# Gates of three dense tiles scattered into a cleared HBM matrix, in place of one-hot products

## The chip, the cores and the metric

The kernel runs on one core of a Trainium2 chip. The metric is the time of one execution on the device, in microseconds, as the median of a few runs. Engines are called by their names in the profile: PE is TensorE, DVE VectorE, ACT ScalarE, POOL GpSimd, SP SyncE (here a queue that issues DMAs).

## What is computed

One layer of a streaming encoder for 640 tokens: 512 of a prompt and 8 x 16 of running streams, in five tiles of 128 tokens. An attention branch and a gated MLP branch are mixed into the residual; after that comes the part that the change touches, a layer of 16384 small experts ("PEER"). Cut to what matters:

```python
q = (xt @ w_query).reshape(T, PEER_HEADS, 2, PEER_HALF)
s = jnp.einsum('thpd,hpnd->thpn', q, sub_keys)
sv, si = lax.top_k(s, PEER_TOPK)                      # 16 of 128 keys, twice
cand = sv[:, :, 0, :, None] + sv[:, :, 1, None, :]
cand_idx = si[:, :, 0, :, None] * PEER_N_KEYS + si[:, :, 1, None, :]
cv, ci = lax.top_k(cand.reshape(T, PEER_HEADS, 256), PEER_TOPK)
eidx = jnp.take_along_axis(cand_idx.reshape(T, PEER_HEADS, 256), ci, axis=-1)
g = jax.nn.softmax(cv, axis=-1)                       # 8 heads x 16 gates per token
a = jax.nn.gelu(jnp.einsum('thkd,td->thk', expert_u[eidx], xt))
return jnp.einsum('thk,thkd->td', (g * a), expert_v[eidx])
```

So each token has 128 (expert, gate) pairs, 16 in each of 8 heads. The 16 experts of one head are distinct; two heads of a token can pick the same expert, and then both gates count.

## The kernel before

The tiles go in two groups. G1 = (0, 4) takes the gathered way: for each of its tiles 128 indirect DMAs fetch 128 rows of U (8 KB each), a DVE instruction per gather makes the dot products, and 128 more gathers from V are multiplied and added up (`gather_peer`, L721 to L763). That is 512 gathers, all on the POOL queue, spread in the background (`bg`, `tick`) over everything that follows the first query; the rates `RATE_...` say how many per step. G2 = (1, 2, 3) takes the dense way: all 16384 experts are computed for all tokens as products, 32 blocks of 512 experts for U and 64 blocks for V (16 groups of 1024 experts by 4 column blocks), and the activations are multiplied by a matrix of gates, wd[token, expert], which is zero but for 128 entries per token.

The order of the work is: mix of G1, query of G1, mix of G2, query of G2 (four products with `w_q`), then `dense_peer`: LEAD = 12 U blocks first, whose activations are stored to HBM (`ad`), and then groups of V blocks, with further U blocks between them once the stored ones are used up. `gemm` (L190) does every product: it loads weights (`raw`), splits each 128 x 512 piece into a high part on ACT (`whi`, L140) and a low part (`wlo`, L141), and multiplies three times per tile (L206 to L208). The low part is made on DVE; in the two queries every second one is made on POOL (`PLG`, `PLQ` = 2). Small work is put between the steps of `gemm`: `pump` takes pieces from `side`, `tick` from `bg`. A scheduler then sets each engine's order.

The matrix wd is made by `weights` (L767): for each token of a tile, two one-hot matrices are compared out of an iota (the first by 128-digit, times the gate; the second by the lower digit), and their product, contracted over the 128 entries, is that token's 128 x 128 row of wd. Four tokens share a PSUM tile, which ACT copies and SP stores to HBM:

```python
nc.vector.tensor_scalar(a, io128, tr[:, 0, t:t + 1], tr[:, 2, t:t + 1],
                        op0=ALU.is_equal, op1=ALU.mult)
nc.tensor.matmul(pw[:, t - t0, :], a, b, start=True, stop=True)      # L788
nc.sync.dma_start(wd[ti][t0:t0 + 4, :].rearrange("t (i j) -> i t j", i=128), w)
```

One such product is two instructions in the profile, so the three tiles have 768. `routing` (L696) finds the digits beforehand; `h_step` (L801) loads a piece of wd, multiplies it with the activations (L806) and transposes the result for V (L810).

Of the kernel before, what the change touches and what calls it, by code (L numbers as in the profile page):

```python
# [23 lines left out]
SAMPLE = 4  # L24
LEAD = 12
RATE_A = 1.35
RATE_Q = 0.6
RATE_W = 1.2
# [17 lines left out]
ACT_OH = 2  # L46
LOWG = -600
PLG = 2
EL = 4
SP = 1.5  # L50
# [8 lines left out]
def body(tc, A, O):  # L59
    nc = tc.nc  # L60
    with ExitStack() as ctx:
# [34 lines left out]
        def load(src, shape=(128, 512)):  # L96
            t = pools["wk"].tile(list(shape), F32, name=nm("b"), tag="b", bufs=cfg["b"])
            nc.sync.dma_start(t, src)
            return t
# [18 lines left out]
        nc.sync.dma_start(gmix, A["gmix"])  # L118
        kT_all = [slot() for _ in range(2)]
# [65 lines left out]

        def drain():
            while side:
                pump(1)

        def gemm(lhs, k0, K, src, evict, ticks=0, width=512):  # L190
            n = len(lhs)
            accs = [acc() for _ in range(n)]
            for kc in range(K // 2):
# [16 lines left out]
                tick(ticks / 2)  # L210
            for i in range(n):
                evict(i, accs[i])
# [200 lines left out]
        route = {}  # L413

# [22 lines left out]
        nc.sync.dma_start(sinks, A["sinks"])  # L437

        def mix(G, xgT, r1, ticks):
# [51 lines left out]
            for nb in range(4):  # L491
# [4 lines left out]
                gemm(xgT, 0, KC, A["w_in"][BLK_VS + nb], ev_z, ticks)  # L496
            ticks = late_ticks
# [3 lines left out]
            for nb in range(4):  # L501
# [4 lines left out]
                gemm(xgT, 0, KC, A["w_in"][BLK_GB + nb], ev_gb, ticks)  # L506
            hs = [mtile([128, D]) for _ in G]
            for nb in range(4):
                cs = slice(nb * 512, nb * 512 + 512)

                def ev_ga(i, a):
                    nc.scalar.activation(hs[i][:, cs], a, AF.Tanh, scale=h1[i])
                gemm(xgT, 0, KC, A["w_in"][BLK_GA + nb], ev_ga, ticks)

# [63 lines left out]
        def query(G, x2T, r2, x1d, xgd, ticks):  # L578
# [3 lines left out]
            if n == 2:  # L582
                for i, ti in enumerate(G):
                    route[ti] = ([], const.tile([128, 128], F32, name=nm("g")), r2[i], x1d[i], xgd[i])
                    bg.append(gather_peer(ti))
            for nb in range(4):
                sub = load(A["subT"][:, nb * 4:nb * 4 + 4, :], (128, 4, 128))

                def ev_r(i, a):
# [13 lines left out]
                    if n == 2:  # L603
                        side.append(pair_index(R[i], G[i], nb))
                gemm(x2T, 0, KC, A["w_q"][nb], ev_r, ticks)

            def fin():
                for i, ti in enumerate(G):
                    if n == 2:
                        gates(route[ti][1], R[i][2])  # L610
                        yield
                    else:
                        yield from routing(R[i], ti)
            side.append(fin())
# [58 lines left out]
        def pair_index(R, ti, q):  # L673
# [12 lines left out]

        def gates(g, cv):
            gv = g.rearrange("p (h k) -> p h k", h=8)
            nc.vector.tensor_sub(gv, cv, cv[:, :, 0:1].to_broadcast([128, 8, 16]))
            nc.scalar.activation(g, g, AF.Exp)  # L690
            gs = stat(8)
            nc.vector.tensor_reduce(gs, gv, axis=AX.X, op=ALU.add)
            nc.vector.reciprocal(gs, gs)
            nc.vector.tensor_mul(gv, gv, gs.unsqueeze(2).to_broadcast([128, 8, 16]))

        def routing(R, ti):  # L696
            sv, si, cv, ci = R
            sif = stage((128, 8, 2, 16))
            nc.vector.tensor_copy(sif, si)
            abf = stage((128, 2, 8, 16))  # L700
            ijg = stage((128, 3, 128))
            places(ci, abf)
            for p in range(2):
                o = ijg[:, p, :].rearrange("p (h k) -> p h k", h=8)
                for q in range(4):
                    hs = slice(2 * q, 2 * q + 2)
                    lookup(o[:, hs], abf[:, p, hs], sif[:, hs, p, :])
                    yield
            gates(ijg[:, 2, :], cv)
            side.append(weights(ti, ijg))  # L710
            yield
# [53 lines left out]
        wd = {}  # L765

        def weights(ti, ijg):  # L767
            wd[ti] = dr.tile([128, 16384], F32, name=nm("wd"))
            pt = misc((128, 4, 128))
            for c in range(3):  # L770
                nc.tensor.transpose(pt[:, c, :], ijg[:, c, :], ident)
            tr = stage((128, 4, 128))
            nc.scalar.copy(tr[:, 0:3, :], pt[:, 0:3, :])
            nc.vector.tensor_scalar_mul(tr[:, 3, :], tr[:, 1, :], -1.0)
            for t0 in range(0, 128, 4):
                pw = misc((128, 4, 128))
                for t in range(t0, t0 + 4):
                    if t % 2 == 0:
                        ab = slot((128, 4, 128))
                    a, b = ab[:, t % 2 * 2, :], ab[:, t % 2 * 2 + 1, :]  # L780
                    nc.vector.tensor_scalar(a, io128, tr[:, 0, t:t + 1], tr[:, 2, t:t + 1],  # L781
                                            op0=ALU.is_equal, op1=ALU.mult)
                    if t % 4 < ACT_OH:
                        nc.scalar.activation(b, io128, AF.Abs, bias=tr[:, 3, t:t + 1])
                        nc.scalar.activation(b, b, AF.Relu, bias=1.0, scale=-1.0)  # L785
                    else:
                        nc.vector.tensor_scalar(b, io128, tr[:, 1, t:t + 1], None, op0=ALU.is_equal)
                    nc.tensor.matmul(pw[:, t - t0, :], a, b, start=True, stop=True)  # L788
                w = slot((128, 4, 128))
                nc.scalar.copy(w, pw)  # L790
                nc.sync.dma_start(wd[ti][t0:t0 + 4, :].rearrange("t (i j) -> i t j", i=128), w)
# [206 lines left out]
```

## Time and profile before

| | us |
|---|---|
| median of 3 runs | 4015.54 (4014.65 to 4018.94) |
| the profiled execution | 4016.88 |
| its span, first to last instruction | 4015.2 |
| PE busy | 3882.2 (97%) |
| DVE busy | 3179.5 (79%) |
| ACT busy | 1727.2 (43%) |
| POOL busy | 799.2 (20%) |
| DMA, mean rate over the span | 295 GB/s |

Matmuls are pipelined: each lasts some 0.39 us, but the next starts after 0.23 us. So starts that follow each other tell how long PE needs, not the mean duration. The granted clock of PE is 0.989 on average. A line of a helper, such as L140 or L206, stands for the whole kernel; the stretches are told apart by time. The second query runs from about 1553 to 1705 us, the first U blocks from there to 2215 us, the one-hot products from 1850 to 2193 us.

### The profile page before, as it was taken

The numbers are of one execution on the slowest core, as the hardware profiler recorded it, in microseconds if no ns is written. First come the engines' busy times: TensorE is split into PE (matmuls) and PEld (weight loads), VectorE is DVE, ScalarE is ACT, GpSimd is POOL, SyncE is SP. The second block draws the span as 40 slices with busy tenths as digits, with TensorE's granted clock in tenths as the row PEclk, the third lists the DMA queues.
The fourth block names the chain that finished last, engine by engine and source line by source line (L and its number), as shares of the span: only waits on it lengthen the run. The fifth ranks groups of instructions, "written<-read, shape, count | busy, mean of one in ns | idle before, by whom it ended". The sixth has DMA issues, their size and how long they took to land.

```text
span 4015.2 us, 52383 instructions
## 1 busy us (share of the span) xinstructions
PE 3882.2 (97%) x17880; PEld 3173.7 (79%) x17880; DVE 3179.5 (79%) x5470; ACT 1727.2 (43%) x3338; POOL 799.2 (20%) x668
## 2 busy tenths in 40 slices
PE   5999998999999999999999899999999999999998
PEld 4778886877777888878888777778888888888886
DVE  4655768977676886989997788888887878787878
ACT  4665554434444334335666333333333333333333
POOL 0000104132211213310111122122222222122213
PEclk8999999999999999999999999999999999999999
DMA  8656786698877898567998989898888888888887
GB/s 216 209 184 202 252 254 234 232 338 316 299 278 279 322 331 301 178 233 250 359 326 271 347 321 352 326 358 331 321 333 319 333 330 329 324 329 325 327 325 288
DMA packets 334300, 1182.84 MB, mean 295 GB/s; under 512 B 34608, under 2 KB 95184, under 8 KB 267472
## 3 DMA queue, kind: packets, MB, share of 16 engines
q1 hardware_dynamic: 260304, 642.59, 48.3%
q0 software_dynamic: 73728, 536.90, 34.7%
q8 instruction: 141, 2.31, 0.2%
q14 instruction: 127, 1.04, 0.1%
HBM read 1117.69 MB, written 61.67 MB: 294 GB/s over the span
## 4 chain that ended last, share of the span: by engine, by line
PE 75%; DVE 10%; DMA 10%; issue 3%; ACT 1%; SPq 0%; POOL 0%; DVEq 0%; ACTq 0%; POOLq 0%
PE acc L207 23%; PE acc L206 23%; PE acc L208 23%; DVE wlo L141 3%; DMA b<-wd 3%; PE pm L788 2%; DMA gb<-in_U,idx 1%; DVE gb L732 1%; DVE xa L737 1%; DMA raw<-in_w_in 1%; DMA gb<-in_V,idx 1%; DMA raw<-in_w_out 1%; PE pm L810 1%; PE pm L301 1%; DVE S L670 1%
## 5 line engine op out<-in xcount | busy, mean ns | idle before, releaser
L206 PE MATMUL acc<-whi,m 128*128 128x512 f32 (+1 forms) x5232 | 2065.4, 395 | 40.6 <-ACT whi L140 40.6
L207 PE MATMUL acc<-wlo,m 128*128 128x512 f32 (+1 forms) x5232 | 2049.9, 392 | 39.8 <-DVE wlo L141 38.1
L208 PE MATMUL acc<-whi,m 128*128 128x512 f32 (+1 forms) x5232 | 2042.7, 390 | 0.0
L140 ACT CAST whi<-raw 128x512 fp32r<-128x512 f32 (+1 forms) x1888 | 1156.5, 617 | 1999.0 <-PE acc L208 1643.0
L141 DVE TENSOR_TENSOR wlo<-raw,whi 128x512 fp32r<-128x512 f32 (+1 forms) x1824 | 1229.5, 692 | 572.4 <-ACT whi L140 568.3
L207 PEld LDWEIGHTS acc<-wlo,m 128*128 128x128 f32 x5232 | 989.2, 189 | 249.1 <-DVE wlo L141 54.5
L206 PEld LDWEIGHTS acc<-whi,m 128*128 128x128 f32 x5232 | 988.8, 189 | 243.1 <-ACT whi L140 42.8
L208 PEld LDWEIGHTS acc<-whi,m 128*128 128x128 f32 x5232 | 988.4, 189 | 201.0
L732 DVE SCALAR_TENSOR_TENSOR gb<-gb,xa 128x2048 f32<-128x2048 f32 x256 | 586.1, 2289 | 68.6 <-DMA gb<-in_U,idx 61.1
L737 DVE SCALAR_TENSOR_TENSOR xa<-gb,hw,xa 128x2048 f32<-128x2048 f32 x239 | 568.2, 2378 | 48.3 <-DMA gb<-in_V,idx 43.2
L746 POOL DMA_INDIRECT gb<-in_V,idx x239 | 310.1, 1297 | 1226.0 <-ACT whi L140 301.3
L746 POOL DMA_INDIRECT gb<-in_U,idx x256 | 331.2, 1294 | 1103.2 <-ACT whi L140 394.9
L141 POOL TENSOR_TENSOR wlo<-raw,whi 128x512 fp32r<-128x512 f32 x64 | 86.9, 1359 | 248.8 <-ACT whi L140 240.6
L788 PEld LDWEIGHTS pm<-s 128*128 128x128 f32 x768 | 101.1, 190 | 20.3 <-ACT s L785 13.6
L781 DVE TENSOR_SCALAR s<-io,S 128x128 f32<-128x128 f32 x384 | 115.9, 345 | 1.1 <-DMA wd<-s 1.1
L839 DVE TENSOR_TENSOR s<-s,acc 128x512 f32<-128x512 f32 x180 | 112.9, 681 | 3.3 <-PE acc L208 3.3
L788 PE MATMUL pm<-s 128*128 128x128 f32 x768 | 111.3, 280 | 1.4 <-ACT s L785 1.1
L141 DVE TENSOR_TENSOR m<-pm,m 128x512 fp32r<-128x512 f32 (+1 forms) x142 | 93.9, 665 | 8.9 <-ACT m L140 7.6
L140 ACT CAST m<-pm 128x512 fp32r<-128x512 f32 (+1 forms) x142 | 79.6, 564 | 28.1 <-PE pm L810 14.6
L790 ACT COPY s<-pm 128x512 f32<-128x512 f32 x96 | 56.5, 589 | 53.0 <-PE pm L788 50.6
L810 PE MATMUL pm<-ident,b 128*128 128x128 f32 x384 | 58.3, 275 | 13.1 <-DVE b L806 12.0
L806 DVE TENSOR_TENSOR b<-b,b 128x512 f32<-128x512 f32 x36 | 24.9, 693 | 56.4 <-DMA b<-wd 48.7
(187 smaller groups left out, 1696.8 us busy)
## 6 DMA issues: line engine op xcount, KB each, us to landing
raw<-in_UT SPq DMA_DIRECT2D x256, 512.0 KB
raw<-in_VP SPq DMA_DIRECT2D x256, 512.0 KB
raw<-in_w_in SPq DMA_DIRECT2D x224, 512.0 KB
raw<-in_w_out SPq DMA_DIRECT2D x64, 512.0 KB
raw<-in_w_q SPq DMA_DIRECT2D x64, 512.0 KB
wd<-s SPq DMA_DIRECT2D x96, 256.0 KB
b<-wd SPq DMA_DIRECT2D x96, 256.0 KB
raw<-in_w_pa SPq DMA_DIRECT2D x32, 512.0 KB
```

The lines of the kernel that those rows point to most:

```text
L140: mark[0] = nc.scalar.copy(hi, src).ins
L141: (E or nc.vector).tensor_sub(lo, src, hi.bitcast(F32))
L206: nc.tensor.matmul(o, xh, hi, start=(k == 0), stop=False)
L207: nc.tensor.matmul(o, xh, lo, start=False, stop=False)
L208: nc.tensor.matmul(o, xl, hi, start=False, stop=(k == K - 1))
L732: q = nc.vector.scalar_tensor_tensor(t, t, 1.0, xg, op0=ALU.mult, op1=ALU.mult, accum_out=dots[:, j:j + 1])
L737: q = nc.vector.scalar_tensor_tensor(y, t, hw[:, j:j + 1], y, op0=ALU.mult, op1=ALU.add)
L746: d = nc.gpsimd.indirect_dma_start(out=t, out_offset=None, in_=src, in_offset=bass.IndirectOffsetOnAxis(ap=idx[j // 32][:, j % 32:j % 32 + ...
L781: nc.vector.tensor_scalar(a, io128, tr[:, 0, t:t + 1], tr[:, 2, t:t + 1], op0=ALU.is_equal, op1=ALU.mult)
L788: nc.tensor.matmul(pw[:, t - t0, :], a, b, start=True, stop=True)
L810: nc.tensor.transpose(pt[:, j, :], w[:, j * 128:j * 128 + 128], ident)
L839: nc.vector.tensor_add(y[i, nb], x1, ps)
```

## The change

wd is now written in three steps. Twelve DMAs of 2 MB (`clear`, issued on SP in the mix of G1) write zeros from one SBUF tile into all of wd. `entries` takes the place of `routing`: for two heads at a time it computes, on DVE, the index token x 16384 + expert of each entry, and the gates. Then 384 indirect DMAs on POOL (3 tiles x 8 heads x 16 entries) each add one element per token to wd in HBM: 128 elements of 4 bytes, an accumulating write. The 16 of one head need no order among each other; each waits for the 16 of the head before in its tile, since two heads may name the same expert. The first load of wd in `dense_peer` waits for the last head. `weights` and `routing` are gone. LEAD goes from 12 to 16, RATE_W from 1.2 to 1.28, the queue's descriptor memory from 8192 to 4096 bytes per partition. The core of the diff:

```diff
-LEAD = 12
+LEAD = 16
-RATE_W = 1.2
+RATE_W = 1.28
+SC = 2.2
...
+        def scatter_tick(n=SC):
+            owed[0] = owed[0] + n if pend else 0.0
+            while owed[0] >= 1.0 and pend:
+                owed[0] -= 1.0
+                ti, idx, g, h, k = pend.pop(0)
+                d = nc.gpsimd.indirect_dma_start(
+                    out=wd[ti].rearrange("t (e o) -> (t e) o", o=1),
+                    out_offset=bass.IndirectOffsetOnAxis(ap=idx[:, h * 16 + k:h * 16 + k + 1], axis=0),
+                    in_=g[:, h * 16 + k:h * 16 + k + 1], in_offset=None, compute_op=ALU.add)
...
+                behind(d.ins, rounds[ti][-2])
+                rounds[ti][-1].append(d.ins)
...
                 tick(ticks / 2)
+                scatter_tick()
...
+        def clear(n, c):
+            if n == 2:
+                w = wd[G2[c // 4]][:, c % 4 * 4096:c % 4 * 4096 + 4096]
+                d = nc.sync.dma_start(w.rearrange("t (k e) -> t k e", k=8),
+                                      zero.unsqueeze(1).to_broadcast([128, 8, 512]))
+                rounds[G2[c // 4]][0].append(d.ins)
...
+        def entries(R, i, ig, q):
+            f = pair(R, q)
+            c = slice(32 * q, 32 * q + 32)
+            nc.vector.scalar_tensor_tensor(f[:, 5], f[:, 4], 128.0, f[:, 5], op0=ALU.mult, op1=ALU.add)
+            nc.vector.tensor_scalar(ig[0][:, c].rearrange("p (h k) -> p h k", h=2), f[:, 5], toff, None, op0=ALU.add)
+            yield
+            gates(ig[1][:, c], R[2][:, 2 * q:2 * q + 2])
+            ready.append((G2[i], *ig))
+            if len(ready) == 3:
+                for h in (2 * q, 2 * q + 1):
+                    pend.extend((*r, h, k) for r in ready for k in range(16))
+                ready.clear()
+            yield
...
-                    w = load(wd[G[i]][:, s * 512:s * 512 + 512])
+                    w = load(wd[G[i]][:, s * 512:s * 512 + 512], before=rounds[G[i]][-1])
...
                     if s == LEAD - EL:
+                        drain()
+                        scatter_tick(len(pend))
                         side.extend([late(0), late(1)])
```

The scheduler's order shows where the scatters stand. On POOL, in the second query, before: low parts of the weights (`wlo`, L141) with a gather (`gb`, L746) after every third or fourth.

```order
L141 TENSOR_TENSOR wlo_3140_14253<-raw_3136_14237,whi_3139_14252 128x512
L141 TENSOR_TENSOR wlo_3145_14281<-raw_3141_14265,whi_3144_14280 128x512
L141 TENSOR_TENSOR wlo_3152_14321<-raw_3148_14305,whi_3151_14320 128x512
L746 DMA gb_3156_14349<-in_V,idx_1360_5802 128x2048
L141 TENSOR_TENSOR wlo_3161_14368<-raw_3157_14352,whi_3160_14367 128x512
L141 TENSOR_TENSOR wlo_3166_14396<-raw_3162_14380,whi_3165_14395 128x512
```

The same engine and stage now (`wd_4` to `wd_6` are the matrices of the tiles 1 to 3, L210 is the scatter, L148 the low part, L799 the gather):

```order
L148 TENSOR_TENSOR wlo_3212_14588<-raw_3208_14572,whi_3211_14587 128x512
L210 DMA wd_5_99<-s_3067_13903,s_3066_13902 2097152x1 x14
L148 TENSOR_TENSOR wlo_3219_14628<-raw_3215_14612,whi_3218_14627 128x512
L210 DMA wd_5_99<-s_3067_13903,s_3066_13902 2097152x1 x2
L210 DMA wd_4_98<-s_3065_13901,s_3064_13900 2097152x1 x6
L148 TENSOR_TENSOR wlo_3224_14656<-raw_3220_14640,whi_3223_14655 128x512
L799 DMA gb_3227_14680<-in_V,idx_1363_5821 128x2048
L210 DMA wd_4_98<-s_3065_13901,s_3064_13900 2097152x1
L148 TENSOR_TENSOR wlo_3232_14699<-raw_3228_14683,whi_3231_14698 128x512
L210 DMA wd_4_98<-s_3065_13901,s_3064_13900 2097152x1 x7
```

Some seven scatters stand ahead of each low part; from the first scatter to the last of these low parts there are 112 scatters, 18 low parts and 5 gathers.

On POOL, in the U blocks, before, nothing but gathers stands, from the last low part on:

```order
L141 TENSOR_TENSOR wlo_3306_15091<-raw_3302_15075,whi_3305_15090 128x512
L141 TENSOR_TENSOR wlo_3311_15119<-raw_3307_15103,whi_3310_15118 128x512
L746 DMA gb_3375_15283<-in_V,idx_1360_5802 128x2048
L746 DMA gb_3383_15326<-in_V,idx_1360_5802 128x2048
L746 DMA gb_3401_15425<-in_V,idx_1360_5802 128x2048
```

On POOL now, in U blocks 2 to 4 (counted from 0):

```order
L210 DMA wd_4_98<-s_3065_13901,s_3064_13900 2097152x1 x19
L799 DMA gb_3570_16278<-in_V,idx_1363_5821 128x2048
L210 DMA wd_4_98<-s_3065_13901,s_3064_13900 2097152x1 x6
L210 DMA wd_5_99<-s_3067_13903,s_3066_13902 2097152x1 x16
L210 DMA wd_4_98<-s_3065_13901,s_3064_13900 2097152x1 x2
L799 DMA gb_3588_16383<-in_V,idx_1363_5821 128x2048
L210 DMA wd_4_98<-s_3065_13901,s_3064_13900 2097152x1 x2
L799 DMA gb_3599_16445<-in_V,idx_1363_5821 128x2048
L799 DMA gb_3617_16550<-in_V,idx_1363_5821 128x2048
L210 DMA wd_4_98<-s_3065_13901,s_3064_13900 2097152x1 x3
L210 DMA wd_5_99<-s_3067_13903,s_3066_13902 2097152x1 x16
L210 DMA wd_6_100<-s_3069_13905,s_3068_13904 2097152x1 x16
```

By U block, from the first: 14, 0, 45, 45, 43, 3, 16, 30, 34 and 40 scatters, with 5, 4, 3, 2, 4, 10, 7, 6, 5 and 4 gathers. On PE, at the same time, before, with the one-hot products (L788) between the products of a U block:

```order
L788 MATMUL pm_4010_18422<-s_4011_18423 128x128 x2
L207 MATMUL acc_3979_18272<-wlo_4021_18468,m_2804_12696 128x512
L788 MATMUL pm_4010_18422<-s_4012_18432 128x128
L208 MATMUL acc_3979_18272<-whi_4020_18467,m_2805_12697 128x512
L788 MATMUL pm_4010_18422<-s_4012_18432 128x128
L206 MATMUL acc_3980_18273<-whi_4020_18467,m_2806_12698 128x512
L207 MATMUL acc_3980_18273<-wlo_4021_18468,m_2806_12698 128x512
```

and now:

```order
L244 MATMUL acc_3802_17531<-wlo_3847_17764,m_2807_12715 128x512
L245 MATMUL acc_3802_17531<-whi_3846_17763,m_2808_12716 128x512
L243 MATMUL acc_3803_17532<-whi_3846_17763,m_2809_12717 128x512
L244 MATMUL acc_3803_17532<-wlo_3847_17764,m_2809_12717 128x512
L245 MATMUL acc_3803_17532<-whi_3846_17763,m_2810_12718 128x512
```

The one-hot products are gone from it and the U block's own stand without a gap. On SP the first load of wd stands among the weight loads of U block 10 (before, near those of U block 7), and waits for all eight of the POOL queue's semaphores. Every POOL DMA, gather or scatter, waits for the eighth before it on these semaphores.

## Rows read from the trace of the kernel before

**Rows 1.** The page: busy time of each engine, and the chain by engine.

```profile
PE 3882.2 (97%) x17880; PEld 3173.7 (79%) x17880; DVE 3179.5 (79%) x5470; ACT 1727.2 (43%) x3338; POOL 799.2 (20%) x668
...
PE 75%; DVE 10%; DMA 10%; issue 3%; ACT 1%; SPq 0%; POOL 0%; DVEq 0%; ACTq 0%; POOLq 0%
```

**Rows 2.** Windows, U blocks: length, busy us (instructions) per engine, clock, DMA share, GB/s.

```profile
1700.00:1748.00 48.00, 48.00 (x230) 39.86 (x229) 38.83 (x86) 18.48 (x31) 9.24 (x8) 1.00 0.71 254
1748.00:1850.00 102.00, 96.87 (x422) 78.06 (x421) 99.89 (x291) 41.12 (x68) 4.81 (x3) 1.00 0.57 180
1850.60:2192.80 342.20, 340.84 (x1857) 286.24 (x1857) 319.39 (x744) 236.11 (x623) 53.67 (x46) 1.00 0.97 330
```

**Rows 3.** Timeline of PE among the one-hots: start, length, what.

```profile
1879.65 0.39 PE L206 MATMUL acc<-whi,m 128*128 128x512 f32 x1
...
1881.46 0.39 PE L208 MATMUL acc<-whi,m 128*128 128x512 f32 x1
...
1884.72 1.16 PE L788 MATMUL pm<-s 128*128 128x128 f32 x8
1885.64 0.47 PE L206 MATMUL acc<-whi,m 128*128 128x512 f32 x1
```

**Rows 4.** Groups of the one-hots' instructions: count, busy us, mean ns, idle before.

```profile
L788 PE MATMUL pm<-s 128*128 128x128 f32 x768 | 111.3, 280 | 1.4 <-ACT s L785 1.1
L781 DVE TENSOR_SCALAR s<-io,S 128x128 f32<-128x128 f32 x384 | 115.9, 345 | 1.1 <-DMA wd<-s 1.1
L787 DVE TENSOR_SCALAR s<-io,S 128x128 f32<-128x128 f32 x192 | 55.4, 289 | 0.0
```

**Rows 5.** Gathers on POOL: ns min/median/max; then the query stage, then the one-hots.

```profile
L746 POOL DMA_INDIRECT gb<-in_U,idx x256: 932/1257/3613, 636.9 to 3270.9; - x128
L746 POOL DMA_INDIRECT gb<-in_V,idx x239: 933/1252/3520, 1525.6 to 3886.4; - x120
...
L141 POOL TENSOR_TENSOR wlo<-raw,whi 128x512 fp32r<-128x512 f32 x31 | 41.4, 1335 | 80.3 <-ACT whi L140 80.2
L746 POOL DMA_INDIRECT gb<-in_V,idx x11 | 19.1, 1740 | 12.6 <-DVE wlo L141 6.2 <-ACT whi L140 5.2 <-issue 0.8
...
L746 POOL DMA_INDIRECT gb<-in_V,idx x47 | 54.6, 1162 | 363.2 <-ACT whi L140 165.7 <-DVE s L781 118.0 <-DVE wlo L141 24.3
```

**Rows 6.** Timeline of POOL in the second query, and DVE beside one gather.

```profile
1560.54 1.29 POOL L141 TENSOR_TENSOR wlo<-raw,whi 128x512 fp32r<-128x512 f32 x1 [2.57 <-ACT whi L140]
...
1600.43 2.83 POOL L746 DMA_INDIRECT gb<-in_V,idx  x1 [0.15 <-issue]
...
1629.62 0.95 POOL L746 DMA_INDIRECT gb<-in_V,idx  x1
...
1703.12 1.63 POOL L141 TENSOR_TENSOR wlo<-raw,whi 128x512 fp32r<-128x512 f32 x1 [2.79 <-ACT whi L140]
...
1598.95 3.48 DVE L737 SCALAR_TENSOR_TENSOR xa<-gb,hw,xa 128x2048 f32<-128x2048 f32 x1 [1.31 <-ACT whi L140]
1867.56 2.35 DVE L737 SCALAR_TENSOR_TENSOR xa<-gb,hw,xa 128x2048 f32<-128x2048 f32 x1
```

**Rows 7.** Chain: a store's landing; then the DMA queues: packets, MB, share.

```profile
1750.25 4.87 DMA ad<-S
...
q1 hardware_dynamic: 260304, 642.59, 48.3%
q0 software_dynamic: 73728, 536.90, 34.7%
```

**Rows 8.** First mix: the chain's longest wait, and a window.

```profile
59.58 27.20 DMA raw<-in_w_in
...
120.00:140.00 20.00, 20.00 (x93) 15.78 (x92) 10.79 (x23) 12.87 (x29) 0.00 (x0) 1.00 0.76 236
```

**Rows 9.** Two windows of the V blocks without U blocks.

```profile
2400.00:2440.00 40.00, 40.00 (x186) 33.15 (x185) 37.21 (x43) 12.85 (x22) 9.47 (x7) 1.00 0.89 338
2440.00:2480.00 40.00, 37.77 (x170) 30.21 (x169) 32.84 (x36) 12.15 (x21) 10.66 (x7) 1.00 0.87 312
```

More of the change, by code (lines that the diff above doesn't have):

```diff
@@ L94, in evs, with load @@
             return pools["wk"].tile(list(shape), F32, name=nm("e"), tag="e", bufs=cfg["e"])
-        def load(src, shape=(128, 512)):
+        def load(src, shape=(128, 512), before=None):
             t = pools["wk"].tile(list(shape), F32, name=nm("b"), tag="b", bufs=cfg["b"])
-            nc.sync.dma_start(t, src)
+            d = nc.sync.dma_start(t, src)
+            if before:
+                behind(d.ins, before)
             return t
@@ L184, in pump, with behind @@
                         side.pop(0)
+        G1, G2 = (0, SAMPLE), (1, 2, 3)
+        wd = {ti: dr.tile([128, 16384], F32, name=nm("wd")) for ti in G2}
+        pend = []
+        owed = [0.0]
+        rounds = {ti: [[]] for ti in G2}
+        def behind(ins, before):
+            for p in before:
+                tc.add_manual_dep(ins, p.name, mybir.DependencyInfo(
+                    mybir.DependencyClass.Sync, mybir.DependencyReason.DATA), reason="same element")
+        def scatter_tick(n=SC):
[7 more added lines that the diff above has]
+                    in_=g[:, h * 16 + k:h * 16 + k + 1], in_offset=None, compute_op=ALU.add)
+                key = f"wd{ti}_{h}"
+                if k:
+                    tc.declare_no_dep(d.ins, group=key, reason="the 16 experts of a head are distinct")
+                else:
+                    rounds[ti].append([])
+                tc.add_to_no_dep_group(key, d.ins)
+                behind(d.ins, rounds[ti][-2])
+                rounds[ti][-1].append(d.ins)
         def drain():
@@ L413, in body @@
         route = {}
+        ready = []
         def prep(G, xgT, r1, order):
@@ L585, in query @@
                     bg.append(gather_peer(ti))
+            else:
+                ig = [(slot((128, 128), I32), slot((128, 128))) for _ in G]
             for nb in range(4):
@@ L608, in fin @@
                 for i, ti in enumerate(G):
[L609 to L614, printed above, removed]
+                    gates(route[ti][1], R[i][2])
+                    yield
+            if n == 2:
+                side.append(fin())
         def top16(v, ix, s, w):
@@ L763, in gather_peer @@
             finish(ti, y, gbuf())
[L765 to L791, printed above, removed]
-                yield
         def dense_peer(G, x2T, r2, x1d):
```

46 lines of the change are left out of this document (22 added, 24 removed).

## The prediction

> **What bounds the kernel now.** I read the page's busy shares first, then its chain, then the stretch that the change touches. TensorE is busy for 3882 of 4015 us and three quarters of the chain are its multiplications [rows 1], so whatever takes work from TensorE shortens the kernel, as long as nothing else becomes late. The windows show where the one-hot products stand [rows 2]: from 1850.6 to 2192.8 us, among the first-layer blocks U. There TensorE has no idle time to speak of (340.84 of 342.20 us), VectorE is at 319 us, the DMA engines at 0.97. GpSimd is busy there for 53.67 us only. Over the whole span it has 799 us of work [rows 1]. It is the engine that the change loads.
>
> Two units are needed. A 512-column product follows the one before it after 0.226 us (eight steps from 1879.65 to 1881.46), so one U block for three tiles, 16 x 9 = 144 products, takes 32.7 us of TensorE at a granted clock of 1.00, the 2.4 GHz level. Eight one-hot products take 0.92 us (1884.72 to 1885.64), 0.115 us each [rows 3].
>
> **What the change removes.** 768 one-hot instructions on TensorE [rows 4] at 0.115 us are 88 us. The other way round: 342.2 us less the other 1857 - 768 = 1089 instructions [rows 2] at 0.227 us leaves 95 us. I take 90. They stand on the path, since TensorE is full there. VectorE loses 115.9 + 55.4 us of comparisons [rows 4], ScalarE its half of them and 96 copies, the SP queue 96 stores. These lie beside TensorE and give nothing themselves, with one exception: from 1748 to 1850 us the table lookups keep VectorE at 99.89 of 102 us and TensorE does 422 instructions, about 6 us less than it could [rows 2]. Spread over more blocks, they may give those 6 us back. Gain: 96 us.
>
> **What it adds, small items.** Twelve clears of 2 MB, put into the first mix, replace stores of the same 25 MB. At 0.76 DMA share and 236 GB/s [rows 8] 2 MB are some 6 us of the DMA engines per block of 96 products, 22 us, and weights are loaded ahead; the only long wait there, 27.2 us at 59.58, stands before the first clear. I take 3 us, between 0 and 15. Four more U blocks are computed ahead, so twelve more activations go to HBM and back (6 MB) and 16 more second-layer blocks stand without a U block between them. Such blocks sometimes lose products to DMA (170 instead of 186 in 40 us [rows 9]); I take 4 us, between 0 and 15. Routing in four pieces instead of one adds small VectorE instructions, less than the comparisons that leave.
>
> **What it adds on GpSimd: the term that decides.** 384 scatters of 128 elements, all between the second block of the second query and U block 9. No row shows a scatter or an accumulating DMA. The nearest rows are the indirect gathers, which also make one entry per partition for 128 partitions: 0.93 us at least, 1.25 us at the median, 1.16 us on average among the one-hots and 1.74 us in the query stage [rows 5]. Call the time of one S. GpSimd works in order, and two things behind the scatters are on the path.
>
> *Query stage.* Half the low parts of the weights (wlo) are made on GpSimd, one for every 18 products. The order shows 112 scatters and 5 gathers among the last 18 of them. Before, 32 of these stood at 1560.54 to 1703.12 us, 4.6 us apart [rows 6], so 18 have 83 us. Now GpSimd needs 112 S + 18 x 1.335 + 5 x 1.3 = 112 S + 30.5 us. At S = 1.25 that is 170 us, 87 too many; five wlo tiles made ahead hide at most 10. Stall: 77 us.
>
> *U blocks 2 to 9.* The order has 256 scatters and 41 gathers here, against 8 x 32.7 = 262 us of TensorE. A late gather holds VectorE, whose multiply-add for it stands in order ahead of the next wlo, and so TensorE. Two gathers are kept in hand, some 12 us. With 1.16 us for both kinds, as in this stage before, GpSimd needs 345 us: stall 345 - 262 - 12 = 71 us. Besides, each head's scatters of a tile wait for the head before. At 15 of 21 such turns ten or more other DMAs lie between; at six there are none to four, and a landing shows. The smallest store shown landed in 4.87 us [rows 7]; I add 4 us for each of the six, 24 us, between 0 and 60.
>
> *The SP queue.* The first load of the scattered matrix waits for the last scatters, and the weights of U block 10 stand behind it. It is late by the same lag, which is counted already.
>
> **Sum.** 77 + 71 + 24 + 3 + 4 - 96 = +83 us on the profiled execution's 4016.9 us. That execution lies 1.3 us over the median of the runs, 4015.5; on the median it gives 4098, and I say **4095 us**, 2.0% slower. With both values of S written out, the stall in the blocks is 112 S - 62 and 256 S - 226 us (neither below 0) and the rest -65. At S = 0.93 the stalls are 42 and 12, the sum is -11 and the time 4005. At S = 1.74 they are 133 and 219: 4303. No change falls at about S = 0.96.
>
> **A rule against the row.** A gather took 2.83 us at 1600.43, beside a VectorE instruction over 2048 elements that itself took 3.48 us instead of 2.35, and 0.95 us at 1629.62 beside short ones [rows 6]. So S depends on what VectorE does at that moment, and five or so of the long ones stand in every U block. The Trainium skill (GPSIMD Engine Reference, 8. Key points) says that GpSimd shares its SBUF interfaces with VectorE and contends with instructions that have two SBUF inputs. The trace agrees with it (2.83 against 0.95 us); if it held for most scatters, 1.74 us would be their time, the 4303 us above.
>
> **Rivals.**
> 1. *The scatter is a cheap instruction (faster).* An entry of 4 bytes could cost GpSimd less than one of 8 KB, or most scatters could stand beside short VectorE instructions, as the 0.95 us gather does, and the six turns could hide in the idle time of U blocks 0, 1 and 5. Then without the 24 us the sum is -89 plus the stalls: S = 0.93 gives 3981, S = 0.75 gives -89 + 22 = 3949, S = 0.55 the full gain, 3927. It decides below S = 1.02. For it: short instructions fill VectorE in the query stage, and GpSimd idles in U blocks 0, 1, 5 and 6. Against it: the median of 1.25.
> 2. *No change.* S within 0.03 of the break-even, 4008 to 4024.
> 3. *The DMA engines bind, not GpSimd (much slower).* Every scatter waits until the eighth DMA before it on that queue has landed. A packet of the load queue takes 48.3% x 16 x 4015 us / 260304 = 119 ns of an engine [rows 7]. If each of a scatter's nine small packets per engine lets one such pass, and costs as much itself, a scatter takes 2.1 us of a ring: stalls 173 and 312 us, time about 4435. Against it: 96 stores in 49152 runs of 512 bytes passed between 1850 and 2190 us beside everything else, at a share of 0.97 [rows 2].
> 4. *VectorE lock*: S near 1.74 as above, 4200 to 4303.
>
> That the products are not gone can be left out: they are absent in the order.
>
> **How the numbers follow.** Forecast (S from 1.0 to 1.45, 4025 to 4195): 0.44. Cheap scatter, 3927 to 4005: 0.35. No change: 0.07. S from 1.45 to 1.75, the fourth rival and its approach: 0.08. DMA bound, above 4303: 0.06. That makes slower 0.58, faster 0.35, same 0.07, where 0.2%, 8 us, is about what a measurement of this kernel can tell from no change. The range for 8 in 10 must take in most of the cheap case and the upper half of the forecast: 3940 leaves out some 0.08 below, 4235 some 0.10 above. The forecast's own range is 4025 to 4195.
>
> **What would show it.** The scatters' mean time on GpSimd: above 1.1 us for the forecast, below 0.95 for the first rival. In the query stage GpSimd's share near 10 tenths and TensorE or its loads waiting for GpSimd's wlo; in U blocks 2 to 9 VectorE waiting for gathers, and SP waiting before its first load of wd. If GpSimd's time per scatter is near 1 us and it waits on DMA instead, the third rival. The gain: one-hots gone, and U blocks 33 us apart wherever nothing stalls. The forecast is wrong if the scatters fit into GpSimd's idle time, or if the late gathers have more slack than two in hand give.

## The result, and the profile after

The changed kernel takes 4471.7 us (median of 4 runs, 4469.1 to 4484.2) beside 4017.0 us of the kernel before on the same chip: a ratio of 1.114 (95% interval 1.1126 to 1.1153). It is slower, as forecast, but by 455 us and not by 80; the time lies far above the range.

The page of the changed kernel: busy times, three rows of the 40 slices, the software queue of the gathers and scatters. They answer to [rows 1, 7].

```profile
PE 3876.1 (87%) x17103; PEld 3146.3 (70%) x17103; DVE 3045.3 (68%) x5059; ACT 1583.0 (35%) x2867; POOL 1463.5 (33%) x1054
...
PE   6999999999999984575165489998999999999998
...
POOL 0000132222222268848868821121122222222222
PEclk8999999999999997887587789999999999999999
...
q0 software_dynamic: 129024, 537.12, 35.0%
```

The loss lies in slices 15 to 24: POOL goes up to 8 tenths, PE falls to between 1 and 8. Ahead of them and behind them the rows look as before. The windows say the same (length, busy us and instructions of PE, PEld, DVE, ACT, POOL, clock, DMA share, GB/s); the second row answers to the second of [rows 2]:

```profile
1600.00:2600.00 1000.00, 538.21 (x2072) 425.52 (x2071) 416.35 (x1155) 182.57 (x298) 769.30 (x467) 0.76 0.53 129
...
1748.00:1850.00 102.00, 55.82 (x193) 43.13 (x192) 30.57 (x118) 15.78 (x28) 88.48 (x57) 0.75 0.40 74
...
2600.00:2700.00 100.00, 100.00 (x452) 82.75 (x451) 71.08 (x73) 38.10 (x63) 18.70 (x16) 0.99 0.89 323
```

In 1000 us TensorE issues 2072 instructions, which at 0.227 us are 470 us of work. The DMA engines are at 0.53 on average; in this stretch a gather landed 6.0 us after its issue (median; 8.5 us over the whole kernel) and a scatter after 3.1 us, so they don't bind.

The scatter's row on POOL, which answers to [rows 5], with what the engine waited for ahead of it; then the groups on POOL from the first scatter to the last:

```profile
L210 POOL DMA_INDIRECT wd<-s,s x384: 1558/1564/3662, 1625.8 to 2586.0; - x192
...
  issue: 113.7, 372
  DVE s L672: 5.5, 1
  DMA wd<-s,s: 3.5, 7
...
L210 POOL DMA_INDIRECT wd<-s,s x383 | 667.1, 1742 | 125.3 <-issue 113.4 <-DVE s L672 5.5 <-DMA wd<-s,s 3.5
L799 POOL DMA_INDIRECT gb<-in_V,idx x56 | 65.0, 1161 | 84.5 <-DVE wlo L148 24.1 <-ACT whi L147 19.4 <-DVE s L764 13.5
L148 POOL TENSOR_TENSOR wlo<-raw,whi 128x512 fp32r<-128x512 f32 x18 | 33.4, 1856 | 0.0
```

A scatter occupies GpSimd for 1.56 us at the least and 1.74 us on average, and each is followed by 0.30 us of issue: 2.04 us. For DMA it waited only 3.5 us in all. Scatters, gathers and low parts together are 667 + 113 + 65 + 33 = 878 of 960 us: GpSimd is all but full there. The timeline shows the beat, 1.88 us from start to start (answers to [rows 6]):

```profile
1694.02 1.58 POOL L210 DMA_INDIRECT wd<-s,s  x1 [0.30 <-issue]
1695.90 1.57 POOL L210 DMA_INDIRECT wd<-s,s  x1 [0.30 <-issue]
1697.78 1.56 POOL L210 DMA_INDIRECT wd<-s,s  x1 [0.30 <-issue]
```

Who waits, from 1600 to 2600 us (us in total, times, longest):

```profile
DVE xa L790 <- DMA gb<-in_V,idx: 356.9, 33, 48.4
...
PE acc L244 <- DVE wlo L148: 339.0, 25, 43.9
...
PE acc L244 <- POOL wlo L148: 122.7, 14, 24.2
```

The first two are one chain: a gather stands behind scatters, VectorE's multiply-add waits for it, the wlo behind that waits, and so TensorE. The third is the query stage. Both chains were in the prediction. TensorE after such a wait, and the window of the products that follow it:

```profile
1708.16 0.80 PE L244 MATMUL acc<-wlo,m 128*128 128x512 f32 x1 [9.64 <-POOL wlo L148]
...
1712.59 0.63 PE L245 MATMUL acc<-whi,m 128*128 128x512 f32 x1
1713.02 0.63 PE L243 MATMUL acc<-whi,m 128*128 128x512 f32 x1
...
1713.99 0.40 PE L243 MATMUL acc<-whi,m 128*128 128x512 f32 x1
1714.22 0.40 PE L244 MATMUL acc<-wlo,m 128*128 128x512 f32 x1
...
1708.16:1713.80 5.64, 5.64 (x14) 4.44 (x15) 1.13 (x6) 0.75 (x2) 5.06 (x4) 0.52 0.79 270
```

After 9.64 us without work the products follow each other at 0.43 us, at a granted clock of 0.52, the 1.2 GHz level, and at 0.23 us again from 1713.8 on.

### The profile page after: what moved, and what is told of

The parts are those of the page before. It is cut to its first block, busy times and chain, and to the rows that moved or that the text cites. A ratio compares the mean times of both kernels' runs of the same rounds, so it can differ in the third digit from the quotient of the medians.

```text
span 4469.8 us, 49992 instructions
## 1 busy us (share of the span) xinstructions
PE 3876.1 (87%) x17103; PEld 3146.3 (70%) x17103; DVE 3045.3 (68%) x5059; ACT 1583.0 (35%) x2867; POOL 1463.5 (33%) x1054
## 3 DMA queue, kind: packets, MB, share of 16 engines
q0 software_dynamic: 129024, 537.12, 35.0%
## 4 chain that ended last, share of the span: by engine, by line
PE 31%; POOL 8%; DMA 7%; issue 4%; DVE 4%; ACT 0%; SPq 0%; DVEq 0%; POOLq 0%; ACTq 0%
PE acc L244 10%; PE acc L245 10%; PE acc L243 10%; POOL wd L210 7%; DMA b<-wd 2%; DMA gb<-in_U,idx 2%; DMA gb<-in_V,idx 1%; DVE wlo L148 1%; DVE gb L785 1%; DVE xa L790 1%; PE pm L835 1%; DMA wd<-s,s 1%; DVE s L864 1%; POOL gb L799 0%; DMA m<-in_V,idx 0%
## 5 line engine op out<-in xcount | busy, mean ns | idle before, releaser
L244 PE MATMUL acc<-wlo,m 128*128 128x512 f32 (+1 forms) x5232 | 2088.1, 399 | 513.6 <-DVE wlo L148 389.2
L243 PE MATMUL acc<-whi,m 128*128 128x512 f32 (+1 forms) x5232 | 2089.7, 400 | 41.2 <-ACT whi L147 41.2
L245 PE MATMUL acc<-whi,m 128*128 128x512 f32 (+1 forms) x5232 | 2073.8, 396 | 0.0
L148 DVE TENSOR_TENSOR wlo<-raw,whi 128x512 fp32r<-128x512 f32 (+1 forms) x1824 | 1217.4, 689 | 671.8 <-ACT whi L147 668.3
L244 PEld LDWEIGHTS acc<-wlo,m 128*128 128x128 f32 x5232 | 1009.7, 193 | 748.9 <-DVE wlo L148 418.0
L243 PEld LDWEIGHTS acc<-whi,m 128*128 128x128 f32 x5232 | 1007.8, 193 | 252.9 <-ACT whi L147 43.4
L245 PEld LDWEIGHTS acc<-whi,m 128*128 128x128 f32 x5232 | 1009.5, 193 | 206.7
L210 POOL DMA_INDIRECT wd<-s,s x384 | 668.7, 1741 | 125.6 <-issue 113.7
L799 POOL DMA_INDIRECT gb<-in_U,idx x256 | 326.9, 1277 | 1144.1 <-DVE wlo L148 402.9
L799 POOL DMA_INDIRECT gb<-in_V,idx x239 | 305.1, 1277 | 910.7 <-DVE wlo L148 402.3
L148 POOL TENSOR_TENSOR wlo<-raw,whi 128x512 fp32r<-128x512 f32 x64 | 97.1, 1519 | 196.3 <-ACT whi L147 190.0
L148 DVE TENSOR_TENSOR m<-pm,m 128x512 fp32r<-128x512 f32 (+1 forms) x142 | 93.9, 664 | 9.5 <-ACT m L147 8.3
L846 ACT ACTIVATE S<-acc,stats 128x512 f32<-128x512 f32 x96 | 63.8, 688 | 49.3 <-DVE S L715 37.7
L432 POOL TENSOR_SCALAR_AFFINE_SELECT b<-b 128x512 f32<-128x512 f32 x8 | 9.1, 1144 | 213.4 <-DMA b<-in_wsT 203.2
```

The costliest lines, as they stand in the source:

```text
L148: (E or nc.vector).tensor_sub(lo, src, hi.bitcast(F32))
L210: d = nc.gpsimd.indirect_dma_start(out=wd[ti].rearrange("t (e o) -> (t e) o", o=1), out_offset=bass.IndirectOffsetOnAxis(ap=idx[:, h * 16 ...
L243: nc.tensor.matmul(o, xh, hi, start=(k == 0), stop=False)
L244: nc.tensor.matmul(o, xh, lo, start=False, stop=False)
L245: nc.tensor.matmul(o, xl, hi, start=False, stop=(k == K - 1))
L799: d = nc.gpsimd.indirect_dma_start(out=t, out_offset=None, in_=src, in_offset=bass.IndirectOffsetOnAxis(ap=idx[j // 32][:, j % 32:j % 32 + ...
```

## The experiments

Theory A: the loss is GpSimd's time for 384 scatters in a stretch that has no room for it. Against it stand: other parts of the change cost it; each scatter costs a fixed amount wherever it stands; and, for the size of the price, adding, direction or number of elements. Times below stand beside 4012 to 4021 us of the kernel before, run on the same chip with them. Runs 3 to 7 and 10 are one execution each and have no interval; the others are medians of four.

**1. No scatters.**

```diff
-                d = nc.gpsimd.indirect_dma_start(out=wd[ti]..., compute_op=ALU.add)
```

> The changed kernel with the 384 scatters left out and all else kept: the clears, the routing in pieces, sixteen U blocks ahead (the three dense tiles' expert gates stay zero, so their expert term is left out of the output). Theory A, the scatters' time on GpSimd is the whole loss (384 of them at 1.56 us busy and 0.30 us of issue, more beside VectorE's work): 3900 to 3950 us, by my sum 3928 (4017 less 96 plus 7), and TensorE's waits for GpSimd's wlo and VectorE's waits for gathers fall back to the size they have in the kernel before. Theory B, the routing in pieces, the clears or the four more U blocks ahead cost a large part: over 4100 us, with TensorE still waiting between 1600 and 2600 us.

3980.0 us, a ratio of 0.991 (0.9892 to 0.9933), 30 us above theory A's range. The first load of wd waits here for the clears alone. From 1600 to 2110 us TensorE waits 21 us for VectorE's low parts and no longer for GpSimd's, and VectorE waits 11 us for gathers. TensorE does the work for which the changed kernel needs 1000 us in 510:

```profile
1600.00:2110.00 510.00, 474.19 (x2075) 387.60 (x2074) 424.72 (x1152) 181.80 (x297) 118.58 (x84) 0.96 0.72 257
```

So the scatters cost 490 us, and nothing else in the change costs on that scale. Where it lies can be read from the stores of U activations, whose rows give count, ns, and the first and last start. The kernel before, this run, the changed kernel:

```profile
L823 SPq DMA_DIRECT2D ad<-S x36: 319/332/1376, 1750.3 to 2215.5; - x36
...
L838 SPq DMA_DIRECT2D ad<-S x48: 319/430/1505, 1765.2 to 2290.1; - x48
...
L848 SPq DMA_DIRECT2D ad<-S x48: 319/423/1296, 1924.2 to 2784.2; - x48
```

From this run to the changed kernel: 159.0 us up to the first store (the query stage), 335.1 us from there to the last of 16 blocks, and -0.5 us behind it (1686.1 against 1685.6 us to the span's end). Against the kernel before, with its four missing blocks put in at 32.7 us each: +14.9, -71.1 and +17.2 us. But 3980 is not the 3928 of my sum: 52 us are still to be explained (12).

**2. One tile by scatters**, the other two by one-hot products, LEAD 12.

```diff
+        SCT = (3,)
-SC = 2.2
+SC = 1.4
```

> A mixture: tile 3's gates by scatters (128 of them, 1.4 a step), tiles 1 and 2 by one-hot products as before, twelve U blocks ahead as before. Theory A (a capacity: loss only where the scatters exceed GpSimd's free time): 128 scatters at 2.07 us are 265 us of GpSimd, spread over the query blocks and eight U blocks of about 32 us, so most are free; a third of the one-hots' 90 us is gained, 3985 to 4010 us. Theory C (every scatter delays the gather or the wlo queued behind it, whatever is free): 128 times the slope seen with all of them, about 1.4 us each, 4017 - 30 + 180 = about 4165 us; 4100 or more.

4162.7 us, 1.036 (1.0344 to 1.038): theory C's number, and A's is missed. The windows show a clump, a pause and a clump:

```profile
1640.00:1800.00 160.00, 87.47 (x344) 68.83 (x343) 69.32 (x297) 27.92 (x48) 132.33 (x85) 0.77 0.39 80
1800.00:1860.00 60.00, 60.00 (x283) 49.80 (x282) 48.65 (x148) 25.96 (x42) 8.56 (x8) 1.00 0.77 274
1860.00:2020.00 160.00, 91.61 (x376) 73.23 (x374) 96.81 (x287) 45.09 (x79) 130.72 (x68) 0.79 0.47 108
```

GpSimd is busy for 132 and 131 of 160 us in the clumps and for 9 of 60 us between them. Free time in a pause doesn't help the work that stands behind a clump. Whether it is the scatter or where it stands is tested by 8.

**3. Writing in place of adding, and 4. a gather of single elements.**

```diff
-                    in_=g[:, h * 16 + k:h * 16 + k + 1], in_offset=None, compute_op=ALU.add)
+                    in_=g[:, h * 16 + k:h * 16 + k + 1], in_offset=None)
```

> The changed kernel with scatters that write in place of adding (where two heads choose the same expert, one of the two gates is left out). Theory D1, adding is what makes a scatter dearer on GpSimd than a gather: its mean busy time falls from 1.74 to about 1.1 us, and the kernel's time to 4020 to 4150 us. Theory D2, the price is that of building 128 small writes, adding or not: 1.7 us busy, 4440 to 4490 us.

> The changed kernel with each scatter replaced by a gather of 128 single elements from the cleared matrix, with the same offsets and in the same places (the three tiles' gates are left out of the output). Theory E1, the direction matters (a write to HBM at offsets costs GpSimd more than a read): about 1.1 us busy each, as the gathers of rows have, and 4020 to 4150 us. Theory E2, the size or number of the pieces matters: 1.6 to 1.75 us busy each, as the scatters, and 4430 to 4490 us.

4276.8 us and 4270.2 us. The scatters' rows (3, then 4) and the software queue of 3; then, of 3, the scatters' group on POOL and the stores of U activations:

```profile
L210 POOL DMA_INDIRECT wd<-s,s x384: 966/972/3159, 1622.5 to 2382.9; - x192
...
L211 POOL DMA_INDIRECT sink<-wd,s x384: 940/944/3188, 1621.7 to 2379.0; - x192
...
q0 software_dynamic: 86016, 537.12, 32.9%
...
L210 POOL DMA_INDIRECT wd<-s,s x384 | 439.1, 1143 | 126.0 <-issue 112.9 <-DVE s L672 5.5 <-DMA wd<-s,s 4.2
...
L848 SPq DMA_DIRECT2D ad<-S x48: 319/422/1106, 1860.0 to 2580.3; - x48
```

Adding makes the scatter dearer: the median falls from 1.564 to 0.972 us as soon as the write doesn't add, and a read of single elements has nearly the same 0.944 us. Direction and size of the pieces don't matter to it; the gathers of whole rows took 0.93 us at the least. Nor does the number of packets explain it. An adding scatter brings (129024 - 73728) / 384 = 144 of them and a plain one 32, but a gather of rows brings 73728 / 512 = 144 as well. The gathers whose rows I took were the right price for the wrong operation.

For the kernel, adding is 195 of the 490 us. The other 297 us stay in run 3, where a scatter is busy for 1.14 us on average, about what I had taken. So both times lie above what I expected: 0.29 us of issue come on top, and 384 x 1.44 us don't fit either.

**5. Half the elements.**

```diff
-ap=idx[:, h * 16 + k:h * 16 + k + 1] ... in_=g[:, h * 16 + k:h * 16 + k + 1]
+ap=idx[0:64, h * 16 + k:h * 16 + k + 1] ... in_=g[0:64, h * 16 + k:h * 16 + k + 1]
```

> The changed kernel with every scatter cut to the first 64 of its 128 partitions (the gates of the other 64 tokens of the three tiles are left out). Theory F1, GpSimd pays for each element: busy falls from 1.74 us to between 0.8 and 1.1 us, and the kernel to 4000 to 4150 us. Theory F2, GpSimd pays a fixed price for the instruction: busy 1.5 to 1.75 us, and 4430 to 4490 us.

4413.0 us; the row, the group on POOL and the stores of U activations:

```profile
L210 POOL DMA_INDIRECT wd<-s,s x384: 1398/1411/3568, 1626.1 to 2527.5; - x192
...
L210 POOL DMA_INDIRECT wd<-s,s x384 | 609.7, 1588 | 125.1 <-issue 114.0 <-DVE s L672 5.5 <-DMA wd<-s,s 2.5
...
L848 SPq DMA_DIRECT2D ad<-S x48: 319/423/910, 1906.3 to 2725.3; - x48
```

Half the elements save 0.15 of 1.56 us. The price is nearly fixed, as F2 said, though the time is 17 us below F2's range.

**6. Half the heads**, 192 scatters.

```diff
+                if h >= 4:
+                    continue
```

> The changed kernel with the scatters of heads 0 to 3 alone, 192 in place of 384, each as before (the gates of heads 4 to 7 of the three tiles are left out). Theory A (capacity): my sum with 180 scatters at 2.07 us against the same 288 us that hide them, less 65: 4037 us; 4000 to 4090. Theory C (each scatter costs the same 1.4 us): 4200 us, half-way between the kernel without scatters and the changed one.

4218.1 us: half the loss, and near C's number. The first store of a U block stands at 1919.1 us, 5 us ahead of the changed kernel's: the heads 0 to 3 are those that crowd the query stage, and only the U blocks lose less. My 288 us of cover belong to the stretch in which the scatters stand; with fewer scatters the stretch is shorter, and so is the cover. In the query stage there are as many scatters as before, so all of the saving is in the U blocks (87 us lost there in place of 335). That is where theory A's 4037 fails.

**7. Low parts on VectorE.**

```diff
-PLQ = 2
+PLQ = 0
```

> The changed kernel with the second query's lo halves all on VectorE (PLQ 0), so that nothing of TensorE's path is queued behind the scatters there. Theory G1, GpSimd's queue of scatters sets the time: it ends only some 33 us earlier (18 lo halves of 1.86 us), and so does the kernel, 4420 to 4470 us; TensorE's 123 us of waits for GpSimd's lo halves turn up as waits for VectorE or before the wd loads. Theory G2, the lo halves' waits are a loss of their own: 4350 us or less.

4443.4 us, G1. The 123 us of waits for GpSimd's wlo are gone, and the kernel gains 28: TensorE's waits for VectorE's wlo grow from 339 to 444 us, as the gathers behind the same scatters are late instead.

**8. One tile, paced.** As 2, but each scatter is bound to the newest copy of a weight block, none stands in the query blocks, LEAD 14.

```diff
+                after(d.ins)
-                scatter_tick()
+                scatter_tick(0.0 if pl[0] else SC)
```

> Tile 3's gates by 128 scatters, tiles 1 and 2 by one-hot products, as in the one-tile run before it, but each scatter is bound to the newest copy of a weight block to hi, and none is written into the query blocks, so that on GpSimd 2 to 4 of them stand between two gathers in place of 6 to 25; fourteen U blocks ahead. Theory H1, the loss of about 1.27 us for each scatter comes from their standing in clumps ahead of the gathers and lo halves that TensorE needs: a step of 4.07 us then holds 1.65 scatters and 0.64 gathers, 1.65 x 1.87 + 0.64 x 1.2 = 3.9 us, which fits, and the kernel comes to 3985 to 4030 us. Theory H2, each scatter costs about 1.27 us wherever it stands (by contention with VectorE or DMA): 4000 + 163 = about 4160 us, as the one-tile run.

4035.5 us, 1.0058 (1.0041 to 1.0075). With the same 128 scatters the kernel is 23 us behind the one before, where run 2 was 148 (two more blocks ahead are the other difference). So 128 scatters cost little in one place and much in another, and a scatter has no fixed price for the kernel: what counts is what stands behind it and whether GpSimd has room in that step.

**9. All scatters, paced over 28 U blocks.**

```diff
-LEAD = 16
+LEAD = 28
-SC = 2.2
+SC = 2.05
```

> All 384 scatters, bound to the newest hi copy and kept out of the query blocks, 2.05 a step, and 28 U blocks ahead in place of 16, so that there are 192 steps for them. Theory H1 (order and capacity): a step holds 2.05 x 1.87 + 0.64 x 1.2 = 4.6 us of GpSimd against 4.07 us of TensorE, 192 x 0.53 = 102 us over the 3980 us of the kernel without scatters, and 0 to 60 us for twelve more blocks ahead: 4080 to 4140 us. Theory H2 (1.27 us each wherever they stand): 3980 + 490 = 4470 us, give or take 40.

(`RATE_C` goes from 1.5 to 1.6 besides, and the scatters are paced as in 8.) 4306.2 us, 1.0744 (1.0725 to 1.0763), between the two. From 2000 to 2700 us, all of it U blocks (window, then POOL's groups):

```profile
2000.00:2700.00 700.00, 575.46 (x2244) 455.84 (x2243) 347.35 (x332) 184.23 (x295) 597.41 (x337) 0.91 0.82 239
...
L210 POOL DMA_INDIRECT wd<-s,s x253 | 486.5, 1923 | 77.1 <-issue 66.1 <-ACT whi L147 5.2 <-DMA wd<-s,s 3.0
L800 POOL DMA_INDIRECT gb<-in_V,idx x84 | 110.9, 1320 | 25.6 <-issue 23.2 <-DMA gb<-in_V,idx 1.2 <-DMA wd<-s,s 1.2
```

486.5 + 66.1 + 110.9 + 23.2 = 686.7 of 700 us: GpSimd sets the pace, and TensorE does 2244 instructions, 509 us of work. H1 holds as a mechanism; its price was too low, since a scatter takes 2.18 us here with its issue and a gather 1.60, not 1.87 and 1.2.

**10. No gathers beside the scatters.**

```diff
-RATE_Q = 0.6
+RATE_Q = 0.0
-PLQ = 2
+PLQ = 0
-                    U(s, RATE_W)
+                    U(s, 0.0 if s < LEAD - EL else RATE_W)
```

> The changed kernel with no gather and no lo half on GpSimd between the second query's start and the twelfth U block (the gathers follow later at the usual pace), so that nothing on TensorE's path stands behind the scatters save the loads of the cleared matrix. Theory H1: TensorE and VectorE run through the query and twelve U blocks as in the kernel without scatters; 384 scatters back to back are 718 us from about 1640 us, to 2360 us, where the twelve blocks end at about 2160 us, so the loss is one wait of about 200 us before the first load, and what the 42 gathers cost later (up to 100 us): 4180 to 4280 us. Theory H2 (the scatters slow VectorE or the DMA by themselves): TensorE also waits between 1640 and 2160 us, and the time is 4350 us or more.

4551.7 us, slower than all others. H1's number is missed. H2's (4350 us or more) is met, and TensorE does wait before 2160 us, but not for H2's reason, as the stretches show. Three windows, and a wait of VectorE from 1600 to 2400 us:

```profile
1640.00:1890.00 250.00, 240.51 (x1078) 197.24 (x1077) 193.14 (x834) 97.10 (x160) 206.23 (x121) 0.98 0.61 129
1900.00:2340.00 440.00, 28.12 (x113) 22.42 (x111) 6.06 (x10) 10.04 (x16) 366.60 (x235) 0.54 0.24 6
...
4400.00:4550.00 150.00, 0.00 (x0) 0.00 (x0) 130.21 (x57) 2.30 (x3) 107.23 (x49) 0.50 0.93 385
...
DVE b L831 <- DMA b<-wd: 460.0, 3, 405.5
```

With GpSimd full of scatters TensorE runs at 240.5 of 250 us: as long as nothing waits for GpSimd, they cost TensorE nothing that shows. Then the first load of wd, which the scheduler's order puts on VectorE near the sixth U block and not after the twelfth as I assumed, holds everything until the last scatter. In the last 150 us TensorE has no product left: these are the gathers put off. The second window also shows the scatter alone, VectorE idle: 366.6 / 235 = 1.56 us, one every 1.87.

**11. One tile, spread wider** (the edit against run 8).

```diff
-LEAD = 14
+LEAD = 20
-SC = 1.65
+SC = 1.05
```

> As the paced one-tile run, with twenty U blocks ahead and 1.05 scatters a step in place of fourteen and 1.65, so that GpSimd has room by the measured prices too (2.09 + 0.30 us for a scatter and 1.4 + 0.3 us for a gather beside the other engines: 1.05 x 2.39 + 0.64 x 1.7 = 3.6 us in a step of 4.07 us; in the run with fourteen it was 5.0 us). Theory H1 (capacity of GpSimd, step by step): the U blocks fall from 42.0 us to about 38 us each, which is 13 x 4 = 52 us of the 4036 us, less up to 35 us for six more blocks ahead: 3985 to 4020 us. Rival H3 (the rest of the loss is VectorE's, by the pieces of routing and one-hots, not the scatters'): U blocks stay at 40 us or more while scatters run, 4030 to 4060 us.

4056.5 us, 1.0098 (1.0077 to 1.0119). The number is H3's; the stretch behind the one-hots shows H1 pure (window, then POOL's groups in it):

```profile
2121.09:2316.93 195.84, 195.84 (x866) 162.16 (x865) 133.86 (x128) 71.45 (x115) 138.57 (x82) 1.00 0.95 320
...
L212 POOL DMA_INDIRECT wd<-gx,ix x51 | 99.7, 1954 | 48.3 <-ACT whi L148 40.5 <-issue 7.5 <-ACT S L894 0.3
L821 POOL DMA_INDIRECT gb<-in_V,idx x31 | 40.3, 1299 | 9.4 <-issue 9.4
```

51 scatters and 31 gathers, and TensorE has no idle time: six U blocks at 32.6 us. Ahead of it, with the other tiles' one-hots and VectorE's routing, blocks take 45 us (46 in run 8), and the six further blocks ahead cost about 20 us behind the last of them. In those blocks of 45 us GpSimd is busy for 201 of 363 us, and its scatters wait 102 us for ScalarE's copies, to which they are bound; in run 8 VectorE still waits 21 us there for gathers. So what 11 still loses is hardly for want of room on GpSimd. That it is VectorE's work and the longer lead was not tested by a run.

**12. Routing later**, without scatters: the pieces that make offsets and gates are written behind the query, fewer a step.

```diff
-                        side.append(entries(R[i], i, ig[i], nb))
+                side.extend(entries(R[i], i, ig[i], q) for q in range(4) for i in range(n))
-SW = 1.6
+SW = 0.6
```

> The kernel without scatters (all else kept, the three tiles' gates left out), with the pieces that turn the chosen places into offsets and gates written behind the last query block, and fewer of them a step in the U blocks (SW 0.6 in place of 1.6). Theory I1, the 52 us by which the kernel without scatters missed my 3928 us are VectorE's backlog from those pieces in the query blocks and the first two U blocks (57 us each in place of 32.6): 3925 to 3950 us. Theory I2, they belong to the sixteen U blocks ahead and the V blocks that follow without U work: 3970 to 3990 us.

3949.7 us, 0.984 (0.9822 to 0.9854): 30 of the 52 us. The stretch that was two U blocks in run 1, first in run 1 and then here, and the stores:

```profile
1765.19:1878.05 112.86, 101.42 (x421) 81.67 (x420) 102.26 (x394) 40.04 (x65) 12.16 (x9) 0.94 0.65 219
...
1765.19:1878.05 112.86, 110.56 (x485) 90.32 (x484) 100.05 (x254) 40.01 (x63) 24.50 (x17) 1.00 0.87 321
...
L838 SPq DMA_DIRECT2D ad<-S x48: 319/430/1011, 1747.3 to 2256.4; - x48
```

Against the kernel before: -3.0 us up to the first store, 509.1 against 596.0 us in the blocks (-86.9), and +20.7 behind. The remaining 20 us lie behind the last block ahead, where the longer lead is the change that is left; run 1 has 17 there.

3950 is about what the change could bring if scatters cost nothing. A third of the one-hots' gain is 29 us, and the paced mixtures end 23 and 40 us behind the kernel before: none that was tried beats it.

## Why the prediction was wrong

By its own steps, on the spans (4015.2 before, 4469.8 after):

| term | forecast, us | measured, us |
|---|---|---|
| one-hots gone and 6 us of VectorE's stretch | -96 | -87 to -90 (run 12) |
| routing in pieces | 0 | +30 (runs 1, 12) |
| clears, four more U blocks ahead | +7 | +17 to +21 |
| scatters, query stage | +77 | +159 |
| scatters, U blocks | +71 | +335 |
| turns of the heads | +24 | near 0 |

**The step that failed is the value of S.** I took 1.25 and 1.16 us from the gathers; a scatter took 1.74 us and 0.30 us of issue. What the formula makes of the measured S (busy and issue), beside the stalls measured against run 1's stores:

| run | S, us | query stage: formula, measured | U blocks: formula, measured |
|---|---|---|---|
| changed kernel | 2.04 | 166, 159 | 296, 335 |
| 5, half the elements | 1.885 | 149, 141 | 257, 294 |
| 3, plain write | 1.44 | 99, 95 | 143, 195 |

So the formula comes within 8 us in the query stage. (By some luck: the trace has 105 scatters ahead of the last low part and not 112, 14 us less, and a low part took 1.86 us and not 1.34, 9 us more.) In the U blocks it is 37 to 52 us short whatever S is: that is a second, smaller error, in the 226 us of cover. The issue time of its 41 gathers, 12 us, is part of it; the rest is open. (Two small sums of the prediction are off too: S = 1.0 gives 4031 and not 4025, and 0.03 of S is 11 us and not 8. Nothing hangs on them.) With run 1's base, 3980 + 462 = 4442 us; the changed kernel has 30 more, which is about that shortfall less the 7 us of the query stage. The lower clock is in the measured stalls: TensorE is busy for 538 us in the first window above, at a granted clock of 0.76, and for 474 us at 0.96 in run 1, for as many instructions.

Why S was too small: adding costs 0.6 us (run 3), and the 0.30 us between one instruction and the next stand in no mean duration; among the gathers of before, which came singly, they lay in idle time. What VectorE's work adds was in the gathers' means already, which lie 0.2 to 0.3 us above their least of 0.93. A scatter as cheap as those gathers would not have saved the forecast: run 3 is that case, at 4277 us.

**Issue time.** The rows that I priced by, [rows 5], give busy time. Back to back, the 0.30 us of issue belong to the price, a sixth of it.

**VectorE beside it.** My rule against the row came out half right: S was 1.74 us busy, the figure of the fourth rival, but by chance: its condition, that most scatters stand beside long VectorE instructions, was not met. With VectorE idle (run 10) the scatter takes 1.56 us, so only some 0.18 us of the mean come from VectorE. The timelines of the changed kernel say the same of its 384 scatters: 228 with VectorE idle took 1.56 to 1.59 us, 90 beside other work of VectorE took 1.71 us on average, and 66 beside a multiply-add over 2048 elements took 2.38 us on average. In run 8 the mean is 2.09 us, with VectorE at 447 of 546 us in the U blocks. The gathers show it one by one (a gather, and VectorE's multiply-add at the same moment):

```profile
2255.38 2.35 DVE L790 SCALAR_TENSOR_TENSOR xa<-gb,hw,xa 128x2048 f32<-128x2048 f32 x1 [18.33 <-DMA gb<-in_V,idx]
...
2255.80 2.77 POOL L799 DMA_INDIRECT gb<-in_V,idx  x1 [0.30 <-issue]
```

The Trainium skill (GPSIMD Engine Reference, 8. Key points) says that the two engines share their SBUF interfaces; the 1.56 to 1.59 us against 2.38 us beside the multiply-add, which reads two tiles, agree with it.

**The rivals.** The cheap scatter falls: no adding scatter of 128 elements took less than 1.55 us. The DMA bound gave the time that is nearest (4435), by chance, and is wrong as a cause: 3.5 us of waits for DMA, scatters that landed in 3.1 us, a DMA share of 0.53. The turns of the heads, my 24 us, fall with it. The clears cost nothing that shows: run 12, which has them, reaches its first U store 3 us ahead of the kernel before.

**Small terms.** Routing in pieces was costed at nothing with the comparisons that leave as its cover. But those left the later U blocks, and the pieces came into the query stage and the first two U blocks (where VectorE has 102 of 113 us in run 1's row above): 18 us and 16 us lie there between runs 1 and 12, 30 us in the time. The lead of sixteen cost 17 to 21 us where I took 4 and 15 at most.

**What was right:** the direction, the places of both stalls, the two chains of waits, the query stage's stall as a function of S (nearly), and the gain of the one-hots.

## What to carry to other kernels

Price an instruction that the trace does not show by its whole beat, busy and issue. Treat an accumulating form as another operation than the read beside it. If a term is multiplied by 368, one such instruction measured beforehand is worth more than a range. An engine with much idle time on average has cover only in the stretch where the new work stands and ahead of what waits for it: count the stretch, and space the work out by a dependency where a scheduler would bunch it. Work moved off an engine's crowded time is free only where it goes, so ask which engine is full there.

## What the runs showed that I had not expected

- An indirect DMA of 128 single elements holds GpSimd for 1.56 us when it adds and 0.97 us when it writes; adding with 64 elements takes 1.41 us. Adding brings 144 packets, writing 32; a gather of 128 rows, also 144 packets, took 0.93 us at the least, so the packets don't set the price.
- 0.30 us lie between such instructions back to back, in gathers, plain writes and adding scatters alike.
- After a wait TensorE's products ran at 0.43 us for about 5 us before they were at 0.23 us again, so a chain of short waits costs more than its idle time: TensorE is busy for 64 us more in the changed kernel's stretch than in run 1's, for as many instructions.
